# A two-branch transformer step on one core: narrower modulation tiles, and a last norm on one engine

## The chip, the core and the metric

The kernel runs on one core of one Trainium2 chip. The core has five engines with instruction streams of their own: TensorE (PE; its weight loads are shown as PEld), VectorE (DVE), ScalarE (ACT), GpSimd (POOL) and SyncE (SP), which here only issues transfers; they wait for each other through semaphores. The metric is the device time in microseconds (us). The kernel before took 1598.36 us, the median of 3 runs (1598.06 to 1599.08).

## What is computed

One layer of a hybrid model is applied to 128 context tokens and 512 latent tokens, 640 rows of 1024 columns in fp32. A conditioning vector for each of the two kinds gives six modulation vectors. Cut to what matters here:

```python
def _layer(x, cond, p, lb, s0):
    mod = jax.nn.silu(cond) @ p['w_ada'] + p['b_ada']          # 1024 -> 6 x 1024
    sh1, sc1, g1, sh2, sc2, g2 = jnp.split(mod[:, None, :], N_MOD, axis=-1)
    mix, s_out = _token_mixer(x * (1 + sc1) + sh1, p, lb, s0)  # conv, gated scan, chunk gating; then W_o
    x = _layernorm(DEEPNORM_ALPHA * x + g1 * mix, p['ln1_g'], p['ln1_b'])
    ffn = _swiglu(x * (1 + sc2) + sh2, p['w_ffn_in'], p['w_ffn_out'])   # 1024 -> 2 x 2816 -> 1024
    x = _layernorm(DEEPNORM_ALPHA * x + g2 * ffn, p['ln2_g'], p['ln2_b'])
    return x, s_out
```

`_layernorm` subtracts the row mean, divides by the row's standard deviation and applies a gain and an offset per column.

## The kernel before

**Products.** Every large product is made of three fp32r matmuls: a weight tile is split into a rounded part (`wh`, ScalarE, L199) and a rest (`wl`, VectorE or POOL, L200), the activations likewise (`split`, L384 on ScalarE and L385 on VectorE), and `mm3` (L216 to L218) or `mm3t` (L221 to L223) multiplies high by high, high by low and low by high into one PSUM tile. The weights come through one queue (L174, on SP) a few tiles ahead.

**Order of the work.** Most of the program is traced as interleaved generators; a scheduler then sets the order on each engine from its own estimates. Where the code stands in `with in_order()`, the instructions of VectorE, ScalarE and POOL keep the order of the program.

**Stages.** The first stage computes four of the twelve 512-column slices of the modulation (L570) while the first weights load. The second, 60 to about 500 us, runs the input projection and the gated scan, and between them the other eight slices, `ada_slice(n)` for n = 4 to 11. Each slice multiplies `silu(cond)` (1024 values for two kinds of token, held as 128x32 blocks, `sil`) by 1024x512 of `w_ada`. `ada_small` (L716) loads it as four tiles of 2 blocks of 128 rows by 512 columns through two buffers (L719, on SP). The matmul (L422) of row block k writes 32 PSUM partitions, at 32 * (k % 4), so the four partition groups collect partial sums of blocks 0 to 3 and then 4 to 7:

```python
j = kc % 4
last = PE.matmul(ps[32 * j:32 * j + 32, :], sil[:, kc, :], t[:, k, :], start=kc < 4, stop=kc >= 4)
```

Then `ada_fin` copies the sum to SBUF, adds the groups by a small matmul (L433 or L439) and adds the bias.

**First norm.** From about 1100 us `o2(t)` computes the second half of the output projection of the 128-row block t (five blocks), adds the residual (L1160, L1161), takes statistics (L1430, L1431) and a reciprocal square root by three Newton steps (`rsqrt_col`, L114 to L122), and gives `nb` (L1434). `x1_apply(t)` normalizes the block on ScalarE (L1439), `x1t(t)` transposes it on TensorE (L1451) and scales it (L1464), followed by the split. In the loop `x1t(t - 1)` follows `o2(t)`.

**Feed-forward part.** `hidden` computes the gated hidden units in groups (its matmuls are L1527 to L1529; `p`, `u` and `fsg` are its intermediate tiles). One step of the generator `x1_resid` is drawn per group: the first scales gain and offset of the first norm by ALPHA (`lgb`, called l1gb in the profile, 128x2048, L1655), and each of five applies them to a block of the residual (`rr`, L1657, L1658).

**Tail.** The last part of the second product runs block by block. `evac` multiplies the PSUM tile by the gate (`rt`, L1693), adds it to `rr` (L1694) and takes statistics (L1696). Then the block's norm follows: mean and variance (L1734), Newton steps, `nb` (L1744), and for each 512-column half either two passes on VectorE (L1741, L1753) or, for six of the ten halves (`by_pool`), one on ScalarE (L1749) and two on POOL (L1750, L1751). Each half is stored by its own transfer (L1755). The scheduler orders the tail.

## Time and profile before

The profiled execution took 1599.31 us (a span of 1597.5 us on the core); the runs' median is 1598.36 us.

| Engine | busy us | share | instructions |
|---|---|---|---|
| PE (TensorE) | 1550.9 | 97% | 10846 |
| DVE (VectorE) | 1148.4 | 72% | 1971 |
| ACT (ScalarE) | 513.5 | 32% | 799 |
| POOL (GpSimd) | 192.3 | 12% | 182 |

148.30 MB moved at a mean of 93 GB/s. The mean granted clock of TensorE was 0.994 of full speed.

How its lines are read: a timeline row gives the start in us, the duration, the engine, the line, the operation, the tile written and those read, the shape and the number of instructions in the row; in brackets stands how long the engine had been idle before, and what released it. Matmuls overlap, so the time one takes from the next is the distance of their starts. A line of waits gives who waited for whom, the total, the number and the longest. In the order rows a matmul counts once where the profile has two records for plain fp32 operands.

### The profile page before, as it was taken

How to read it: one execution, taken by the hardware profiler on the slowest of the kernel's cores; microseconds unless marked ns; L12 is line 12 of the kernel's file. 1: busy time of each engine (PE TensorE's matmuls, PEld its weight loads, DVE VectorE, ACT ScalarE, POOL GpSimd, SP SyncE). 2: the span in 40 equal slices, each digit the busy share in tenths (PEclk: the TensorE clock that was granted, in tenths of full speed). 3: DMA queues.
4: the chain of work that ended last, by engine and by line, in shares of the span. 5: the costliest groups of instructions: out<-in, count | busy, mean ns of one | idle time of the engine just before them, and what ended most of it. 6: DMA issues, size and time to landing. Idle time of an engine off the chain costs nothing.

```text
span 1597.5 us, 26110 instructions
## 1 busy us (share of the span) xinstructions
PE 1550.9 (97%) x10846; PEld 1422.4 (89%) x10846; DVE 1148.4 (72%) x1971; ACT 513.5 (32%) x799; POOL 192.3 (12%) x182
## 2 busy tenths in 40 slices
PE   7999999999999999999999999999899999999995
PEld 4988998888887899999999899997788898898984
DVE  5555456565677999988997563377896685685878
ACT  3333333233333221121222343223643243242441
POOL 1120220322300000000002312430000000000014
PEclk9999999999999999999999999999899999999998
DMA  9632333333222322322222123432133222223221
GB/s 321 207 106 87 88 98 100 99 94 100 70 58 81 91 80 67 89 70 78 68 67 67 53 80 106 159 93 66 48 111 119 66 80 98 62 80 93 62 85 66
DMA packets 197014, 148.30 MB, mean 93 GB/s; under 512 B 4945, under 2 KB 174441, under 8 KB 196640
## 3 DMA queue, kind: packets, MB, share of 16 engines
q1 hardware_dynamic: 195984, 145.24, 30.2%
q8 instruction: 85, 1.39, 0.4%
q10 hardware_dynamic: 912, 1.39, 0.2%
q14 instruction: 33, 0.27, 0.1%
HBM read 140.31 MB, written 6.31 MB: 92 GB/s over the span
## 4 chain that ended last, share of the span: by engine, by line
PE 84%; DVE 7%; DMA 5%; ACT 2%; issue 1%; POOL 0%; SPq 0%; ACTq 0%; DVEq 0%
PE mm L216 15%; PE mm L218 15%; PE mm L217 15%; PE fx L1527 3%; PE fx L1529 3%; PE fx L1528 3%; PE lv L810 3%; PE fy L1527 2%; PE fo L221 2%; PE fo L222 2%; PE fo L223 2%; PE fy L1529 2%; PE fy L1528 2%; DMA adaw<-in_w_ada_dram 2%; PE vps L221 2%; PE vps L223 2%
## 5 line engine op out<-in xcount | busy, mean ns | idle before, releaser
L216 PE MATMUL mm<-mH,wh 128*128 128x320 f32 x1280 | 401.8, 314 | 0.0
L217 PE MATMUL mm<-mL,wh 128*128 128x320 f32 x1280 | 396.4, 310 | 0.0
L218 PE MATMUL mm<-mH,wl 128*128 128x320 f32 x1280 | 396.1, 309 | 0.0
L199 ACT CAST wh<-raw 128x1024 fp32r<-128x1024 f32 (+1 forms) x186 | 185.0, 995 | 534.7 <-PE mm L217 358.4
L200 DVE TENSOR_TENSOR wl<-raw,wh 128x1024 fp32r<-128x1024 f32 (+1 forms) x185 | 220.6, 1193 | 140.2 <-ACT wh L199 140.0
L216 PEld LDWEIGHTS mm<-mH,wh 128*128 128x128 f32 x1280 | 240.3, 188 | 9.0 <-issue 5.5
L217 PEld LDWEIGHTS mm<-mL,wh 128*128 128x128 f32 x1280 | 240.4, 188 | 3.6 <-issue 3.6
L218 PEld LDWEIGHTS mm<-mH,wl 128*128 128x128 f32 x1280 | 240.3, 188 | 0.3
L997 DVE SCALAR_TENSOR_TENSOR ca<-hb,convw,ca 128x328 f32<-128x328 f32 x464 | 229.0, 560 | 0.0
L1527 PE MATMUL fy<-mT,wh 128*128 128x320 f32 x264 | 85.1, 323 | 3.8 <-ACT p L1541 2.5
L1529 PE MATMUL fy<-mT,wl 128*128 128x320 f32 x264 | 83.6, 316 | 0.4 <-DVE wl L200 0.4
L1528 PE MATMUL fy<-mT,wh 128*128 128x320 f32 x264 | 83.0, 315 | 0.3 <-DVE mT L1519 0.3
L199 ACT CAST wh<-S 128x1024 fp32r<-128x1024 f32 x43 | 44.9, 1050 | 91.2 <-issue 34.7
L221 PE MATMUL vps<-wh,mH 128*128 128x256 f32 (+1 forms) x200 | 66.6, 334 | 0.0
L200 POOL TENSOR_TENSOR wL<-raw,wL 128x1024 fp32r<-128x1024 f32 (+1 forms) x3 | 6.8, 2280 | 494.1 <-ACT wL L199 489.5
L223 PE MATMUL vps<-wh,mL 128*128 128x256 f32 (+1 forms) x200 | 65.7, 328 | 0.0
L222 PE MATMUL vps<-wl,mH 128*128 128x256 f32 (+1 forms) x200 | 65.5, 328 | 0.0
L200 DVE TENSOR_TENSOR wl<-S,wh 128x1024 fp32r<-128x1024 f32 x43 | 52.6, 1222 | 17.5 <-ACT wh L199 17.5
L754 POOL TENSOR_SCALAR fT<-fT,oml,lb 128x640 f32<-128x640 f32 x16 | 26.1, 1632 | 322.6 <-ACT fT L751 270.2
L832 DVE TENSOR_TENSOR k<-k,t 128x320 f32<-128x320 f32 x40 | 21.8, 546 | 55.1 <-PE lv L810 54.8
L1527 PEld LDWEIGHTS fy<-mT,wh 128*128 128x128 f32 x264 | 50.7, 192 | 8.5 <-ACT p L1541 5.4
L1527 PE MATMUL fx<-mB,wh 128*128 128x320 f32 x176 | 55.1, 313 | 2.0 <-ACT u L1604 1.3
(406 smaller groups left out, 3413.1 us busy)
## 6 DMA issues: line engine op xcount, KB each, us to landing
raw<-in_w_in_dram SPq DMA_DIRECT2D x96, 512.0 KB
adaw<-in_w_ada_dram SPq DMA_DIRECT2D x48, 512.0 KB
raw<-in_w_ffn_in_dram SPq DMA_DIRECT2D x44, 512.0 KB
raw<-in_w_ffn_out_dram SPq DMA_DIRECT2D x20, 512.0 KB
raw<-in_w_b_out_dram SPq DMA_DIRECT2D x8, 512.0 KB
raw<-in_w_c_out_dram SPq DMA_DIRECT2D x8, 512.0 KB
raw<-in_w_a_out_dram SPq DMA_DIRECT2D x8, 512.0 KB
raw<-in_w_o_dram SPq DMA_DIRECT2D x8, 512.0 KB
```

The costliest lines, as they stand in the source:

```text
L199: S_.copy(h, raw)
L200: le.tensor_tensor(out=lo, in0=raw, in1=h.bitcast(F32), op=ALU.subtract)
L216: PE.matmul(ps, h, aH, start=first, stop=False)
L217: PE.matmul(ps, h, aL, start=False, stop=False)
L218: return PE.matmul(ps, lo, aH, start=False, stop=last)
L221: PE.matmul(ps, aH, h, start=first, stop=False)
L222: PE.matmul(ps, aH, lo, start=False, stop=False)
L223: return PE.matmul(ps, aL, h, start=False, stop=last)
L997: paced(V_.scalar_tensor_tensor(out=ca[:, p_], in0=hb[:, p_.start + j:p_.stop + j], scalar=convw[:, k, j:j + 1], in1=ca[:, p_], op0=ALU.mu ...
L1527: PE.matmul(ps, wh, bh, start=kc == 0 and not add, stop=False, skip_group_check=add)
L1528: PE.matmul(ps, wh, bl, start=False, stop=False, skip_group_check=add)
L1529: PE.matmul(ps, wl, bh, start=False, stop=kc == 3, skip_group_check=add)
```

## The change

It has four parts.

1. **Modulation slices of the second stage.** A tile is now four row blocks by 256 columns, [128, 4, 256] for [128, 2, 512], and each tile's four matmuls, 32x256, go to the four partition groups. There are still four loads of 512 KB a slice, two buffers and the same totals; the rows of a load are 1 KB for 2 KB.
2. **First norm.** `x1t(0)` is called in the middle of `o2(2)`, behind four of its eight k blocks, and not behind `o2(1)`.
3. **l1gb.** The scaling by ALPHA is a ScalarE activation; the constraint that put it behind the last instruction of the stretch in order is gone, and the first draw of the generator is left out, so the residual blocks follow one group later.
4. **Last norm.** All halves are normalized on VectorE, in steps: `rsqrt_col` is now a generator (with the multiplication by -0.5 ahead of the first guess), and `norm2(t)` yields between its steps. `evac` of the next block draws up to three steps after each of its instructions. The tail stands in `in_order()`, so VectorE keeps this order. POOL and ScalarE do nothing there but ScalarE's part of the transfers.

```diff
--- before.py
+++ after.py
@@ -107,18 +107,26 @@
             V_.scalar_tensor_tensor(out=dst, in0=u, scalar=1.5, in1=dst, op0=ALU.add, op1=ALU.mult)
             yield
 
...
+        yield
         V_.tensor_scalar(out=u.bitcast(I32), in0=x[:, 0:1].bitcast(I32), scalar1=1, scalar2=None,
                          op0=ALU.logical_shift_right)
+        V_.tensor_scalar(out=x[:, 1:2], in0=x[:, 0:1], scalar1=-0.5, scalar2=None, op0=ALU.mult)
+        yield
         V_.tensor_scalar(out=dst.bitcast(I32), in0=u.bitcast(I32), scalar1=-1.0, scalar2=float(MAGIC),
                          op0=ALU.mult, op1=ALU.add)
-        V_.tensor_scalar(out=x[:, 1:2], in0=x[:, 0:1], scalar1=-0.5, scalar2=None, op0=ALU.mult)
         for _ in range(3):
+            yield
             V_.tensor_scalar(out=u, in0=dst, scalar1=dst, scalar2=x[:, 1:2], op0=ALU.mult, op1=ALU.mult)
+            yield
             V_.scalar_tensor_tensor(out=dst, in0=u, scalar=1.5, in1=dst, op0=ALU.add, op1=ALU.mult)
 
     def ln_stats(pool, src, mean, rstd, tag):
@@ -409,19 +417,12 @@
 
     def ada_slice(n, pmp, loads, pool, tag):
 
-        fin = ada_mm(n, pmp, loads, pool, tag)[1]
-        fin()
-
-    def ada_mm(n, pmp, loads, pool, tag):
         ps = pmp.tile([P, 512], F32, tag="pm", name="mods")
-        last = None
-        for t, k0, kcs in loads(n):
-            for k in range(kcs):
-                kc = k0 + k
-                j = kc % 4
-                last = PE.matmul(ps[32 * j:32 * j + 32, :], sil[:, kc, :], t[:, k, :],
-                                 start=kc < 4, stop=kc >= 4)
-        return last.ins, lambda: ada_fin(n, ps, pmp, pool, tag)
+        for t, c0, k0 in loads(n):
+            for j in range(4):
+                PE.matmul(ps[32 * j:32 * j + 32, c0:c0 + 256], sil[:, k0 + j, :], t[:, j, :],
+                          start=k0 == 0, stop=k0 == 4)
+        ada_fin(n, ps, pmp, pool, tag)
 
...
@@ -714,11 +715,12 @@
...
     def ada_small(n):
-        for k0 in range(0, KC, 2):
-            t = hp.tile([P, 2, 512], F32, tag="adw", name="adaw2", bufs=2)
-            SP.dma_start(t, w_ada[k0 * P:(k0 + 2) * P, n * 512:(n + 1) * 512].rearrange(
-                "(k p) n -> p k n", p=P))
-            yield t, k0, 2
+        for c0 in (0, 256):
+            for k0 in (0, 4):
+                t = hp.tile([P, 4, 256], F32, tag="adw", name="adaw2", bufs=2)
+                SP.dma_start(t, w_ada[k0 * P:(k0 + 4) * P, n * 512 + c0:n * 512 + c0 + 256].rearrange(
+                    "(k p) n -> p k n", p=P))
+                yield t, c0, k0
 
     def ada_op(n):
         def f():
@@ -1416,7 +1418,7 @@
     xH, xL = X()
...
-    def o2(t):
+    def o2(t, mid=None):
         tsl = slice(t * P, (t + 1) * P)
         ps = newps("ops2")
         stt = st["lbs"][:, t]
@@ -1424,6 +1426,8 @@
         nn = 512 if t < NT - 1 else 256
         for c in range(0, 512, nn):
             for k in range(KC):
+                if k == 4 and mid:
+                    mid()
                 mm3t(ps[:, 0, c:c + nn], oH[:, k, c:c + nn], oL[:, k, c:c + nn], xH[:, k, tsl], xL[:, k, tsl],
                      k == 0, k == KC - 1)
             resid(t, 512 + c, nn, ps[:, 0, c:c + nn], g1b)
@@ -1470,8 +1474,8 @@
 
     w_need(3)
     for t in range(NT - 1):
-        x1_apply(t, o2(t))
-        if t:
+        x1_apply(t, o2(t, (lambda: x1t(0)) if t == 2 else None))
+        if t > 1:
             x1t(t - 1)
     order = in_order()
     order.__enter__()
@@ -1651,8 +1655,7 @@
 
     def x1_resid():
 
-        with tc.issue_after(last.ins):
-            V_.tensor_scalar(out=lgb, in0=lgb, scalar1=ALPHA, scalar2=None, op0=ALU.mult)
+        S_.activation(lgb, lgb, AF.Copy, scale=ALPHA)
         for t in range(NT):
             V_.tensor_tensor(out=rr[:, t], in0=rr[:, t], in1=lgb[:, 0], op=ALU.mult)
             V_.tensor_tensor(out=rr[:, t], in0=rr[:, t], in1=lgb[:, 1], op=ALU.add)
@@ -1660,6 +1663,14 @@
 
     x1r = x1_resid()
     st2 = pe.tile([P, NT, 3, 6], F32, name="st2")
+    norms = []
+
+    def norm_steps(n):
+        while n and norms:
+            n -= 1
+            if next(norms[0], True):
+                norms.pop(0)
+
...
@@ -1675,7 +1686,8 @@
                 hH.append(hs[:, 2 * k - 4])
                 hL.append(hs[:, 2 * k - 3])
             left = hidden(hH[k], hL[k], early.pop(0) if early else None, left)
-            next(x1r, None)
+            if part or k:
+                next(x1r, None)
             gate.clear()
         left()
         if part == 0:
@@ -1688,12 +1700,15 @@
             SP.dma_start(lgb2[:, 1], bcast_row(ln2_b[0]))
         final = part == len(PARTS) - 1
 
-        def evac(t, ps, n0, nn):
+        def evac(t, ps, n0, nn, steps=0):
             tmp = pe.tile([P, nn], F32, tag="rt", name="rt2")
             V_.tensor_tensor(out=tmp, in0=ps, in1=g2b[:, min(t, 1), n0:n0 + nn], op=ALU.mult)
+            norm_steps(steps)
             V_.tensor_tensor(out=rr[:, t, n0:n0 + nn], in0=rr[:, t, n0:n0 + nn], in1=tmp, op=ALU.add)
+            norm_steps(steps)
             if final:
                 V_.bn_stats(st2[:, t, {512: 0, 768: 1}.get(n0, 2)], rr[:, t, n0:n0 + nn])
+            norm_steps(steps)
 
...
-    by_pool = ((0, 0), (1, 0), (2, 0), (2, 1), (3, 0), (3, 1))
-    w_take(2 * len(L_KCS))
-    for t in range(NT):
...
-        for i in cols_:
-            for kc in range(HH - 1 if t == 0 else 0, HH):
-                prod(*i, kc)
-            evac(t, ps[i[0]], *i)
+    def norm2(t):
         mv = pe.tile([P, 2], F32, tag="mv", name="mv2", bufs=2)
         V_.bn_aggr(mv, st2[:, t] if t == NT - 1 else st2[:, t, 0::2])
+        yield
         rs = pe.tile([P, 1], F32, tag="rs2", name="rs2", bufs=2)
-        rsqrt_col(pe, rs, mv[:, 1:2], tag="ln2")
-        for hf in range(2):
+        xs = [rr[:, t, hf * 512:(hf + 1) * 512] for hf in range(2)]
+        for i, _ in enumerate(rsqrt_col_g(pe, rs, mv[:, 1:2], tag="ln2")):
+            if i in (1, 3):
+                V_.scalar_tensor_tensor(out=xs[i // 2], in0=xs[i // 2], scalar=mv[:, 0:1],
+                                        in1=lgb2[:, 0, i // 2 * 512:(i // 2 + 1) * 512], op0=ALU.subtract, op1=ALU.mult)
+            yield
+        dst = y_prompt[0] if t == 0 else y_sample[0, (t - 1) * P:t * P, :]
+        for hf, x in enumerate(xs):
             sl = slice(hf * 512, (hf + 1) * 512)
-            x = rr[:, t, sl]
-            if (t, hf) not in by_pool:
-                V_.scalar_tensor_tensor(out=x, in0=x, scalar=mv[:, 0:1], in1=lgb2[:, 0, sl],
-                                        op0=ALU.subtract, op1=ALU.mult)
-        nb = pe.tile([P, 1], F32, tag="nb2", name="nb2", bufs=2)
-        V_.scalar_tensor_tensor(out=nb, in0=mv[:, 0:1], scalar=-1.0, in1=rs, op0=ALU.mult, op1=ALU.mult)
-        for hf in range(2):
-            sl = slice(hf * 512, (hf + 1) * 512)
-            x = rr[:, t, sl]
-            if (t, hf) in by_pool:
-                S_.activation(x, x, AF.Identity, scale=rs, bias=nb)
-                G_.tensor_tensor(out=x, in0=x, in1=lgb2[:, 0, sl], op=ALU.mult)
-                G_.tensor_tensor(out=x, in0=x, in1=lgb2[:, 1, sl], op=ALU.add)
-            else:
-                V_.scalar_tensor_tensor(out=x, in0=x, scalar=rs, in1=lgb2[:, 1, sl], op0=ALU.mult, op1=ALU.add)
-            dst = y_prompt[0] if t == 0 else y_sample[0, (t - 1) * P:t * P, :]
+            yield
+            V_.scalar_tensor_tensor(out=x, in0=x, scalar=rs, in1=lgb2[:, 1, sl], op0=ALU.mult, op1=ALU.add)
             (SP if hf else S_).dma_start(dst[:, sl], x)
+
+    w_take(2 * len(L_KCS))
+    with in_order():
+        for t in range(NT):
...
+            for i in cols_:
+                for kc in range(HH - 1 if t == 0 else 0, HH):
+                    prod(*i, kc)
+                evac(t, ps[i[0]], *i, 0 if t == NT - 1 and i[0] == 768 else 3)
+            norms.append(norm2(t))
+        norm_steps(1000)
 
 
 # ---- launch: one core; inputs and outputs as the reference has them ----
```

TensorE at the third and fourth tile of the first slice (`adaw` is a tile of w_ada, `mods` the slice's PSUM tile), before:

```order
L216 MATMUL mm<-mH,wh 128x320
L422 MATMUL mods<-adaw_971,sil 32x512 x2
L217 MATMUL mm<-mL,wh 128x320
L218 MATMUL mm<-mH,wl 128x320
L216 MATMUL mm<-mH,wh 128x320
L217 MATMUL mm<-mL,wh 128x320
L218 MATMUL mm<-mH,wl 128x320
L422 MATMUL mods<-adaw_975,sil 32x512 x2
L810 MATMUL lv<-q_850,k_710 64x64 x10
```

and in the change:

```order
L224 MATMUL mm<-mH,wh 128x320
L423 MATMUL mods<-adaw_975,sil 32x256 x4
L225 MATMUL mm<-mL,wh 128x320
L226 MATMUL mm<-mH,wl 128x320
L224 MATMUL mm<-mH,wh 128x320
L225 MATMUL mm<-mL,wh 128x320
L226 MATMUL mm<-mH,wl 128x320
L224 MATMUL mm<-mH,wh 128x320
L225 MATMUL mm<-mL,wh 128x320
L423 MATMUL mods<-adaw_981,sil 32x256 x4
```

Each lone tile has four narrow matmuls for two wide ones; the third tile stands three matmuls earlier, and seven matmuls lie between the two for five.

VectorE at the scaling of l1gb (`S` are sums of weight tiles, `hp` the rest of a hidden group, `u` and `fsg` the group's gate), before:

```order
L200 TENSOR_TENSOR wl<-S_10987,wh 128x1024
L1655 TENSOR_SCALAR l1gb<-l1gb 128x2048
L1590 TENSOR_TENSOR u_10874<-u_10874,fy 128x320
L1657 TENSOR_TENSOR rr<-rr,l1gb 128x1024
L1591 TENSOR_TENSOR fsg<-fsg,u_10874 128x320
L1658 TENSOR_TENSOR rr<-rr,l1gb 128x1024
L385 TENSOR_TENSOR hp<-fsg,hp 128x640
L1211 TENSOR_TENSOR S_11089<-raw 128x512
L1212 TENSOR_TENSOR S_11089<-raw 128x512
L200 TENSOR_TENSOR wl<-raw,wh 128x1024
```

and in the change:

```order
L208 TENSOR_TENSOR wl<-S_11051,wh 128x1024
L1594 TENSOR_TENSOR u_10938<-u_10938,fy 128x320
L1595 TENSOR_TENSOR fsg<-fsg,u_10938 128x320
L1660 TENSOR_TENSOR rr<-rr,l1gb 128x1024
L393 TENSOR_TENSOR hp<-fsg,hp 128x640
L1213 TENSOR_TENSOR S_11150<-raw 128x512
L1214 TENSOR_TENSOR S_11150<-raw 128x512
L208 TENSOR_TENSOR wl<-raw,wh 128x1024
```

The scaling and one of the two passes over `rr` are gone from ahead of `hp` and `wl`. On ScalarE, in the same place, the scaling now stands ahead of the rounding of `hp` and of the next `wh`:

```order
L207 CAST wh<-S_11051 128x1024
L1658 ACTIVATE l1gb<-l1gb 128x2048
L392 CAST hp<-fsg 128x640
L207 CAST wh<-raw 128x1024
L1545 COPY p_11174<-fx 128x320
L1545 COPY p_11189<-fy 128x320
```

Before, it read there:

```order
L199 CAST wh<-S_10987 128x1024
L1541 COPY p_11113<-fx 128x320
L199 CAST wh<-raw 128x1024
L1541 COPY p_11128<-fy 128x320
L199 CAST wh<-raw 128x512
L384 CAST hp<-fsg 128x640
```

The two copies and the smaller rounding come later in exchange, and `hp` earlier.

VectorE in the tail, from the first column half of block 1 to the second (`st` are statistics, `mv` mean and variance of block 0, `rs` its reciprocal root), before:

```order
L1693 TENSOR_TENSOR rt_14610<-fo,g2b 128x512
L1734 BN_AGGR mv_14570<-st_10995 128x2
L1694 TENSOR_TENSOR rr<-rr,rt_14610 128x512
L114 TENSOR_SCALAR ln2x<-mv_14570 128x1
L1741 SCALAR_TENSOR_TENSOR rr<-rr,mv_14570,l2gb 128x512
L115 TENSOR_SCALAR ln2u<-ln2x 128x1
L119 TENSOR_SCALAR ln2x<-ln2x 128x1
L1696 BN_STATS st_10995<-rr 128x6
L117 TENSOR_SCALAR rs_14572<-ln2u 128x1
L121 TENSOR_SCALAR ln2u<-rs_14572,ln2x 128x1
L122 SCALAR_TENSOR_TENSOR rs_14572<-ln2u,rs_14572 128x1
```

and in the change:

```order
L1705 TENSOR_TENSOR rt_14650<-fo,g2b 128x512
L1728 BN_AGGR mv_14652<-st_11059 128x2
L118 TENSOR_SCALAR ln2x<-mv_14652 128x1
L120 TENSOR_SCALAR ln2u<-ln2x 128x1
L122 TENSOR_SCALAR ln2x<-ln2x 128x1
L1734 SCALAR_TENSOR_TENSOR rr<-rr,mv_14652,l2gb 128x512
L1707 TENSOR_TENSOR rr<-rr,rt_14650 128x512
L124 TENSOR_SCALAR rs_14654<-ln2u 128x1
L128 TENSOR_SCALAR ln2u<-rs_14654,ln2x 128x1
L1734 SCALAR_TENSOR_TENSOR rr<-rr,mv_14652,l2gb 128x512
L130 SCALAR_TENSOR_TENSOR rs_14654<-ln2u,rs_14654 128x1
L1710 BN_STATS st_11059<-rr 128x6
```

A second pass (L1734) stands where POOL had one, and the short steps are spread between the long ones; the last two passes (L1741) of block 0 come behind the next `rt`.

More of the change, by code (lines that the diff above doesn't have):

```diff
@@ L108, in rsqrt_g, with rsqrt_col, rsqrt_col_g @@
             yield
-    def rsqrt_col(pool, dst, var, tag):
+    def rsqrt_col(*a, **k):
+        for _ in rsqrt_col_g(*a, **k):
+            pass
+    def rsqrt_col_g(pool, dst, var, tag):
         x = pool.tile([P, 2], F32, tag=tag + "x", name=tag + "x")
@@ L1708, in hybrid_step @@
                         evac(t, slot[t], hf * 512, 512)
-    by_pool = ((0, 0), (1, 0), (2, 0), (2, 1), (3, 0), (3, 1))
-    w_take(2 * len(L_KCS))
-    for t in range(NT):
-        tsl = slice(t * P, (t + 1) * P)
-        cols_ = [(512, 512), (0, 512)]
-        if t == NT - 1:
-            cols_ = [(0, 512), (512, 256), (768, 256)]
-        ps = {n0: bank("fo")[:, 0:nn] for n0, nn in cols_}
-        def prod(n0, nn, kc):
-            o = n0 % 512
-            h, lo = [w[:, kc, o:o + nn] for w in st[f"wL{n0 // 512}"]]
-            mm3t(ps[n0], h, lo, hH[kc][:, tsl], hL[kc][:, tsl], kc == 0, kc == HH - 1)
-        if t == 0:
-            for i in cols_:
-                for kc in range(HH - 1):
-                    prod(*i, kc)
-        for i in cols_:
-            for kc in range(HH - 1 if t == 0 else 0, HH):
-                prod(*i, kc)
-            evac(t, ps[i[0]], *i)
+    def norm2(t):
@@ new lines, in hybrid_step, with prod @@
+    w_take(2 * len(L_KCS))
+    with in_order():
+        for t in range(NT):
+            tsl = slice(t * P, (t + 1) * P)
+            cols_ = [(512, 512), (0, 512)]
+            if t == NT - 1:
+                cols_ = [(0, 512), (512, 256), (768, 256)]
+            ps = {n0: bank("fo")[:, 0:nn] for n0, nn in cols_}
+            def prod(n0, nn, kc):
+                o = n0 % 512
+                h, lo = [w[:, kc, o:o + nn] for w in st[f"wL{n0 // 512}"]]
+                mm3t(ps[n0], h, lo, hH[kc][:, tsl], hL[kc][:, tsl], kc == 0, kc == HH - 1)
+            if t == 0:
+                for i in cols_:
+                    for kc in range(HH - 1):
+                        prod(*i, kc)
+            for i in cols_:
+                for kc in range(HH - 1 if t == 0 else 0, HH):
+                    prod(*i, kc)
+                evac(t, ps[i[0]], *i, 0 if t == NT - 1 and i[0] == 768 else 3)
+            norms.append(norm2(t))
+        norm_steps(1000)
```

## Prediction

> **What bounds the kernel now.** I read the page first: the span, and the engines' shares of the chain that ended last.
>
> ```profile
> span 1597.5 us, 26110 instructions
> PE 84%; DVE 7%; DMA 5%; ACT 2%; issue 1%; POOL 0%; SPq 0%; ACTq 0%; DVEq 0%
> ```
>
> TensorE (PE) carries the chain, so a TensorE microsecond saved, or an idle one closed, comes off the end, except where another engine ends last. Four stretches of the view by windows (length; busy PE, PEld, DVE, ACT, POOL; granted clock; DMA share; GB/s) show where that is.
>
> ```profile
> 10.00:45.00 35.00, 30.97 (x233) 20.59 (x236) 23.09 (x68) 12.07 (x22) 3.91 (x5) 1.00 1.09 353
> 300.00:400.00 100.00, 98.47 (x930) 87.36 (x928) 57.41 (x94) 34.70 (x67) 21.23 (x22) 1.00 0.32 96
> 500.00:700.00 200.00, 200.00 (x1251) 190.85 (x1250) 193.99 (x418) 45.15 (x50) 1.25 (x15) 1.00 0.27 77
> 1545.00:1598.00 53.00, 35.45 (x164) 28.17 (x162) 45.84 (x106) 7.57 (x11) 21.78 (x14) 0.91 0.14 50
> ```
>
> The first is bound by loads, the second and the third (like nearly all of 60 to 1545) by TensorE, the last by VectorE. The change touches stretches of the last two kinds, so each part needs its own ruler. TensorE's waits that bear on it:
>
> ```profile
> PE mods L422 <- DMA adaw<-in_w_ada_dram: 3.8, 7, 2.0
> PE fo L221 <- DVE rt L1693: 2.7, 5, 0.9
> ```
>
> **Part 1, modulation slices.** TensorE's timeline at the first of the eight slices, one later tile, and a visit of the first stage:
>
> ```profile
> 36.28 1.93 PE L570 MATMUL mods<-adaw,sil 128*32 128x256 f32 x32
> 38.14 0.51 PE L648 MATMUL v0a<-wh,mH 128*128 128x256 f32 x2
> ...
> 89.20 1.07 PE L422 MATMUL mods<-adaw,sil 128*32 128x512 f32 x8
> ...
> 94.27 1.05 PE L422 MATMUL mods<-adaw,sil 128*32 128x512 f32 x4
> 95.25 0.41 PE L217 MATMUL mm<-mL,wh 128*128 128x320 f32 x1
> ...
> 96.18 1.05 PE L422 MATMUL mods<-adaw,sil 128*32 128x512 f32 x4
> ...
> 299.40 1.05 PE L422 MATMUL mods<-adaw,sil 128*32 128x512 f32 x4 [1.97 <-DMA adaw<-in_w_ada_dram]
> ```
>
> An instruction leaves two records here, so x8 is the pair of tiles at a slice's start (four instructions, one on each 32-column position), and x4 a tile alone: two instructions on two positions. The pair takes 1.07 and the lone tile 1.05: half the work for the same time. The first stage shows the new shape, 32x256 on all four positions: x32 is 16 instructions, four tiles' worth, and 38.14 - 36.28 = 1.86 us, so 0.465 a tile, where a lone tile now holds TensorE 95.25 - 94.27 = 0.98. All eight slices have two lone tiles; the number of visits stays. Saved: 16 x (0.98 - 0.465) = 8.2; with the pair as the ruler (half of 1.07 less the 0.07 of overlap, 0.50) 16 x 0.48 = 7.7. I take 7.7.
>
> What can take some back is the loads. Two buffers serve four tiles, so the third and the fourth load wait until TensorE has released the first and the second. In the changed order the third tile stands three 128x320 matmuls earlier, but the first tile is released after one of the pair's two halves, some 0.5 us earlier: even. The second is released when it was; the fourth tile is reached by TensorE about 0.5 (shorter third) + 0.15 (two matmuls fewer ahead of it) earlier. How much room there is shows the DMA view of 88 to 100 us, 0.3 us a digit:
>
> ```profile
> DMA  0000020000093998999998200000569899410001
> ```
>
> The third and fourth tile's bytes move from 91.3 to about 94.9, and the fourth is used at 96.18: 1.3 us of room, less 0.65. The rows of a load become 1 KB instead of 2 KB. The 10 to 45 us stretch, where slices with 1 KB rows load beside weights with shorter ones, moved 353 GB/s; two tiles are 1.05 MB, 3.0 us by that, inside the 3.7 that the pair takes here. Seven waits already stand at these tiles, 3.8 us in all, among them the 1.97 in the last row. In that slice (the fifth) one matmul of the first tile was placed 30 us ahead; now the whole first tile and one matmul of the second are, so only the fourth load still waits for a late release and that 1.97 stays about what it is. At the other six places TensorE comes up to 0.65 earlier: 6 x 0.2 for half of them or so, 1.2. **Sum -6.5**; bounds -8.2 (nothing given back) and -3 (0.3 us at all 16 lone tiles, 4.7).
>
> The Trainium skill (DMA: Bandwidth & Descriptors, Specifications) puts the smallest transfer for line rate at 512 B; by it rows of 1 KB cost nothing and this part would be -7.7 or more. The 353 GB/s agrees as far as it goes.
>
> **Part 2, the transposes of block 0 one block later.** TensorE, VectorE and ScalarE there:
>
> ```profile
> 1107.24 1.24 ACT L1439 ACTIVATE rr<-rr,nb,rstd 128x1024 f32<-128x1024 f32 x1 [10.89 <-DVE nb L1434]
> 1108.53 1.09 PE L1451 MATMUL x1T<-ident,rr 128*128 128x128 f32 x8 [1.30 <-ACT rr L1439]
> ...
> 1111.62 0.16 DVE L1434 SCALAR_TENSOR_TENSOR nb<-lbm,rstd 128x1 f32<-128x1 f32 x1
> ...
> 1121.45 1.09 PE L1451 MATMUL x1T<-ident,rr 128*128 128x128 f32 x8
> ```
>
> TensorE stood 1.30 for ScalarE's normalization of block 0. With the transposes seven matmuls later that wait goes. But block 1's transposes keep their place, and need block 1's normalization: nb at 1111.62 comes at the end of a VectorE sequence that runs without a gap from 1107 and doesn't start earlier. 1111.62 + 0.2 + 1.24 puts them at about 1113.1, where TensorE arrives at 1112.5: half the stall is back there, and block 2's (1121.45) hang on VectorE, which now has block 0's split between. **Sum 0**, bounds -1.3 (the whole stall) and +0.5.
>
> **Part 3, scaling l1gb on ScalarE.** The three engines at the start of the feed-forward part:
>
> ```profile
> 1158.12 1.23 DVE L1655 TENSOR_SCALAR l1gb<-l1gb 128x2048 f32<-128x2048 f32 x1 [0.24 <-DMA l1gb<-in_ln_b_dram]
> ...
> 1162.96 0.83 DVE L385 TENSOR_TENSOR hp<-fsg,hp 128x640 fp32r<-128x640 f32 x1 [0.54 <-ACT hp L384]
> ...
> 1164.91 1.22 DVE L200 TENSOR_TENSOR wl<-raw,wh 128x1024 fp32r<-128x1024 f32 x1
> 1160.41 1.05 ACT L199 CAST wh<-raw 128x1024 fp32r<-128x1024 f32 x1 [0.19 <-DMA raw<-in_w_ffn_in_dram]
> 1161.51 0.41 PE L1527 MATMUL fx<-mB,wh 128*128 128x320 f32 x1 [0.29 <-ACT wh L199]
> 1166.18 0.42 PE L1529 MATMUL fx<-mB,wl 128*128 128x320 f32 x1 [2.03 <-DVE wl L200]
> ```
>
> TensorE stands 2.03 for wl, the end of the VectorE queue. Out of that queue go the scaling (1.23) and one of the two rr passes ahead of it (the first call of the generator is skipped, so one full-width pass of 1.22 moves behind). ScalarE gets 128x2048: twice the 1.24 of its 128x1024, less one fixed part, 2.3 us, from about 1158.1 (landing of l1gb) to 1160.4. Then come hp (0.73), wh (1.05, done 1162.0 instead of 1161.4: TensorE's 0.29 wait grows by 0.6). VectorE waits for the scaled l1gb, runs one rr pass 1160.45 to 1161.6, then hp, two sums, and wl from 1163.55 to 1164.75, where it was 1164.91 to 1166.13. TensorE's 2.03 shrinks to what is left behind the grown wait; it goes on at 1164.8 instead of 1166.18. The moved pass falls in a stretch with VectorE slack. **Sum -1.35**; bounds -2.0 (all of the wait) and +0.7 (ScalarE's queue slips and wl gains nothing).
>
> **Part 4, last norm on VectorE.** VectorE's timeline at the tail, POOL's row beside it:
>
> ```profile
> 1556.16 0.69 DVE L1693 TENSOR_TENSOR rt<-fo,g2b 128x512 f32<-128x512 f32 x1
> ...
> 1557.57 0.74 DVE L1741 SCALAR_TENSOR_TENSOR rr<-rr,mv,l2gb 128x512 f32<-128x512 f32 x1
> ...
> 1560.44 0.16 DVE L122 SCALAR_TENSOR_TENSOR rs<-ln2u,rs 128x1 f32<-128x1 f32 x1
> ...
> 1562.09 1.48 DVE L1694 TENSOR_TENSOR rr<-rr,rt 128x512 f32<-128x512 f32 x1
> ...
> 1564.21 0.67 DVE L1693 TENSOR_TENSOR rt<-fo,g2b 128x512 f32<-128x512 f32 x1
> ...
> 1579.80 0.67 DVE L1693 TENSOR_TENSOR rt<-fo,g2b 128x512 f32<-128x512 f32 x1
> ...
> 1586.40 0.24 DVE L1734 BATCH_NORM_AGGREGATE mv<-st 128x2 f32<-128x18 f32 x1
> ...
> 1587.53 1.63 DVE L1741 SCALAR_TENSOR_TENSOR rr<-rr,mv,l2gb 128x512 f32<-128x512 f32 x1
> ...
> 1589.56 0.73 DVE L122 SCALAR_TENSOR_TENSOR rs<-ln2u,rs 128x1 f32<-128x1 f32 x1
> ...
> 1590.63 0.88 DVE L122 SCALAR_TENSOR_TENSOR rs<-ln2u,rs 128x1 f32<-128x1 f32 x1
> ...
> 1591.85 0.99 DVE L122 SCALAR_TENSOR_TENSOR rs<-ln2u,rs 128x1 f32<-128x1 f32 x1
> ...
> 1592.96 1.41 DVE L1753 SCALAR_TENSOR_TENSOR rr<-rr,rs,l2gb 128x512 f32<-128x512 f32 x2
> 1561.72 1.30 POOL L1750 TENSOR_TENSOR rr<-rr,l2gb 128x512 f32<-128x512 f32 x1 [10.20 <-ACT rr L1749]
> ```
>
> VectorE runs from block to block without a gap: 8.05 us from block 1 to block 2, (1579.80 - 1564.21) / 2 = 7.80 after. While POOL works, instructions of VectorE with two operands from SBUF take twice as long: 1.48 for a 0.69 sum, 1.63 for a 0.74 one. The change adds two half-block passes (0.65 each at their cadence), takes away nb (0.08) and the slowing (1.48 - 0.69 = 0.79): 8.05 + 0.43 = 8.5 a block; as the short rsqrt steps now stand between long passes and no longer wait for one another, I take 8.25. The last block starts 8.05 + 15.6 - 3 x 8.25 = 1.1 us late; in it VectorE also has the four passes of block 3, which POOL did: 4 x 0.65, less about 0.4 for one slowed sum, part of which covered short steps. So its statistics end 1.1 + 2.2 = 3.3 late. The final chain was 1594.37 - 1586.40 = 7.97, of which 0.89 is the slowed pass and 2.1 the three slowed Newton steps (0.73, 0.88 and 0.99 for 0.16): 4.95 without POOL, 3.0 less. **Sum +0.3**, bounds -2 (the passes hide all rsqrt waits) and +2 (8.5 a block, and no more from the last).
>
> **Total** -6.5 + 0 - 1.35 + 0.3 = -7.5. The profiled execution took 1599.31 us, 0.95 above the median of the runs, so 1591.8 for such an execution and 1590.9, say **1591**, for the median. About 0.2% (3.2 us) can be told from no change.
>
> **Rivals.** *The loads take the gain (16%).* If the fourth tile's load isn't covered, the gain of the slice turns into the wait beside 299.40: with 0.3 us at each of 16 tiles and parts 3 and 4 at their middle it is 1598.4 - 3 - 1.05 = 1594.3; with part 3's gain lost too, 1595.7. For it: seven waits are there already. Against: 1.3 us of room in the slice shown.
>
> *The loads overturn it (4%).* One mechanism on the other side: each lone tile waits like the one at 299.40, and the weight loads queued behind it on SP come late. It decides from 16w = 3.8 + 7.7 + 1.1 + 3.2, so w = 1 us per lone tile; at the full 1.97 the result is 1598.4 - 7.7 - 1.1 + 31.5 - 3.8, 1617. Against it: the DMA share of 0.32 at 300 to 400 us, and no wait for weights in that stage.
>
> *The clock decides (8%).* TensorE's granted clock falls after idle stretches in the feed-forward start:
>
> ```profile
> 1155.00:1160.00 5.00, 4.74 (x23) 4.74 (x24) 4.76 (x7) 0.89 (x2) 0.00 (x0) 0.68 1.05 321
> ```
>
> A stretch like this one loses 5 x 0.32 = 1.6 us. Parts 2 and 3 move its idle gaps: with two stretches more the result is 1594, with this one gone 1589. The Trainium skill (TensorE: Matmul & The Clock Gate, Part 1) has the gate look through a free-running window, so every earlier microsecond could shift which gap trips it. The runs of before lie within 1.0 us, which speaks against large luck.
>
> *Everything lands (13%).* No wait for loads, block 0's stall gone for good, VectorE's tail 2 shorter: -8.2 - 1.3 - 1.35 - 2, about 1586.
>
> *Tail at its bad end (6%)*, VectorE at 8.5 or more a block: 1593.
>
> **Chances.** The forecast, between 1588.5 and 1593.5, has 53%. Faster by more than 0.2% (below 1595.2) come the forecast, the full gain, 0.06 of the clock's 0.08, 0.04 of the tail's 0.06 and a quarter of the first rival: 0.53 + 0.13 + 0.06 + 0.04 + 0.04 = 0.80. Within 0.2% come the rest of that rival and 0.02 of clock and tail: 0.14. Slower are the overturn and what is left of clock and tail: 0.06. The range 1586 to 1596.5 leaves out the full overturn and a tenth at the ends.
>
> **What would show it.** Part 1: rows of 32x256 x8 (a lone tile) of about 0.5 us and waits for adaw in all below 6 us; wrong if those waits pass 8. Part 2: the 1.30 is gone, and a stall of about 0.6 stands at block 1's transposes. Part 3: wl's 2.03 falls below 0.8, and wh's 0.29 grows. Part 4: no POOL row behind 1552, no sum over 0.8 us on VectorE there, blocks 8.2 to 8.5 apart, a final chain near 5 us. The forecast fails if the span from 60 to 500 us shortens by less than 4 us.

## The result

The changed kernel took 1588.55 us (median of 4 runs, 1587.7 to 1590.29), the kernel before beside it 1598.21: a ratio of 0.9939 with a 95% interval of 0.9927 to 0.9952, that is 7.7 to 11.7 us less. Measured again beside two variants of it, it was 0.9931 (0.9918 to 0.9943). The forecast was 1591, 7.4 us less, with a range of 1586 to 1596.5.

The page of the changed kernel, the same two lines as before:

```profile
span 1587.1 us, 26350 instructions
PE 86%; DVE 7%; DMA 4%; ACT 2%; issue 1%; POOL 0%; ACTq 0%; DVEq 0%
```

The share of loads in the chain fell by one point, and TensorE's rose. To see where the 10.4 us of span went, I cut both traces at the starts of the same instructions and take the difference of the lengths: the first matmul of the gated scan (`lv`), the first of the output projection (`ops`), the first of the feed-forward part (`fx`), the first of its second product (`fo`), the last of its first product (`fx` or `fy`), and the end. The other columns are runs of the experiments below, each with one part alone; each column is a single execution.

| stretch, us | before | after | part 1 alone | part 2 alone | part 3 alone | part 4 alone |
|---|---|---|---|---|---|---|
| start to first lv | 80.90 | 79.80 | 79.85 | 80.27 | 80.39 | 79.98 |
| to first ops (slices) | 1014.16 | 1007.25 | 1007.10 | 1013.42 | 1014.98 | 1015.53 |
| to first fx (first norm) | 29.73 | 29.64 | 29.60 | 29.43 | 29.14 | 29.57 |
| to first fo (l1gb) | 94.59 | 92.56 | 94.42 | 94.34 | 91.41 | 93.17 |
| to last fx or fy | 325.00 | 324.58 | 324.58 | 325.16 | 325.14 | 325.18 |
| to the end (tail) | 53.16 | 53.30 | 53.06 | 53.09 | 53.06 | 53.29 |

The second row carries 6.9 of the 10.4 us, the fourth 2.0, the first 1.1 (code that the change doesn't touch), the fifth 0.4, and the tail gives back 0.1. The terms of the four parts can thus be read apart, which totals that spread over some microseconds don't allow.

**Part 1.** TensorE's timeline at the first slice and at one later third tile, then its waits:

```profile
88.10 1.07 PE L423 MATMUL mods<-adaw,sil 128*32 128x256 f32 x16
...
92.64 0.64 PE L423 MATMUL mods<-adaw,sil 128*32 128x256 f32 x8
93.21 0.41 PE L225 MATMUL mm<-mL,wh 128*128 128x320 f32 x1
...
391.20 0.64 PE L423 MATMUL mods<-adaw,sil 128*32 128x256 f32 x8 [1.36 <-DMA adaw<-in_w_ada_dram]
```

```profile
PE mods L423 <- DMA adaw<-in_w_ada_dram: 2.6, 3, 1.4
PE x1T L1455 <- ACT rr L1443: 1.2, 2, 0.7
```

A lone tile holds TensorE 93.21 - 92.64 = 0.57 us where it held it 0.98; the pair stays at 1.07. Summed over all visits, without the waits ahead of them, the slices hold TensorE 17.5 us for 24.4. The waits for loads didn't grow: seven of 3.8 us became three of 2.6.

**Part 2.** Block 0's transposes and those of block 1 and 2, with the normalization that block 1's wait for:

```profile
1100.66 1.04 PE L1455 MATMUL x1T<-ident,rr 128*128 128x128 f32 x8
...
1103.64 0.16 DVE L1438 SCALAR_TENSOR_TENSOR nb<-lbm,rstd 128x1 f32<-128x1 f32 x1
1103.84 1.24 ACT L1443 ACTIVATE rr<-rr,nb,rstd 128x1024 f32<-128x1024 f32 x1 [1.30 <-DVE nb L1438]
...
1105.14 1.09 PE L1455 MATMUL x1T<-ident,rr 128*128 128x128 f32 x8 [0.71 <-ACT rr L1443]
...
1113.37 1.09 PE L1455 MATMUL x1T<-ident,rr 128*128 128x128 f32 x8 [0.46 <-ACT rr L1443]
```

The stall of 1.30 at block 0 is gone, and 0.71 and 0.46 stand at the next two: 1.17 in all. ScalarE itself waits 1.30 for `nb`, so it is VectorE's statistics that set this pace, and they weren't moved.

**Part 3.** ScalarE, VectorE and TensorE where l1gb is scaled:

```profile
1149.79 1.92 ACT L1658 ACTIVATE l1gb<-l1gb 128x2048 f32<-128x2048 f32 x1 [2.09 <-DMA l1gb<-in_ln_b_dram]
...
1152.23 1.04 ACT L207 CAST wh<-raw 128x1024 fp32r<-128x1024 f32 x1
1154.82 1.22 DVE L208 TENSOR_TENSOR wl<-raw,wh 128x1024 fp32r<-128x1024 f32 x1
1153.32 0.42 PE L1531 MATMUL fx<-mB,wh 128*128 128x320 f32 x1 [0.33 <-ACT wh L207]
...
1156.13 0.38 PE L1533 MATMUL fx<-mB,wl 128*128 128x320 f32 x1
```

The wait of 2.03 us for `wl` is gone altogether, and the one for `wh` is 0.33 where it was 0.29.

**Part 4.** VectorE at the first product sum of blocks 1, 2 and 4, the last statistics, and the last two passes:

```profile
1545.55 0.69 DVE L1705 TENSOR_TENSOR rt<-fo,g2b 128x512 f32<-128x512 f32 x1
...
1553.80 0.67 DVE L1705 TENSOR_TENSOR rt<-fo,g2b 128x512 f32<-128x512 f32 x1
...
1570.28 0.67 DVE L1705 TENSOR_TENSOR rt<-fo,g2b 128x512 f32<-128x512 f32 x1
...
1579.07 0.24 DVE L1728 BATCH_NORM_AGGREGATE mv<-st 128x2 f32<-128x18 f32 x1
...
1582.54 1.42 DVE L1741 SCALAR_TENSOR_TENSOR rr<-rr,rs,l2gb 128x512 f32<-128x512 f32 x2
```

Blocks are 8.25 us apart (8.24 each on to block 4), and the final chain is 1583.96 - 1579.07 = 4.89 us for 7.97.

### The profile page after: what moved, and what is told of

The parts are those of the page before. It is cut to its first block, busy times and chain, and to the rows that moved or that the text cites. A ratio compares the mean times of both kernels' runs of the same rounds, so it can differ in the third digit from the quotient of the medians.

```text
span 1587.1 us, 26350 instructions
## 1 busy us (share of the span) xinstructions
PE 1543.0 (97%) x10974; PEld 1423.8 (90%) x10974; DVE 1148.4 (72%) x1977; ACT 510.2 (32%) x794; POOL 173.8 (11%) x170
## 4 chain that ended last, share of the span: by engine, by line
PE 86%; DVE 7%; DMA 4%; ACT 2%; issue 1%; POOL 0%; ACTq 0%; DVEq 0%
PE mm L224 15%; PE mm L226 15%; PE mm L225 15%; PE fx L1531 3%; PE fx L1533 3%; PE lv L812 3%; PE fx L1532 3%; PE fy L1531 3%; PE fo L229 2%; PE fo L230 2%; PE fo L231 2%; PE fy L1533 2%; PE fy L1532 2%; PE vps L229 2%; PE vps L230 2%; PE vps L231 2%
## 5 line engine op out<-in xcount | busy, mean ns | idle before, releaser
L208 DVE TENSOR_TENSOR wl<-S,wh 128x1024 fp32r<-128x1024 f32 x43 | 52.5, 1222 | 17.5 <-ACT wh L207 17.5
```

Of the source, the lines that this page charges most:

```text
L208: le.tensor_tensor(out=lo, in0=raw, in1=h.bitcast(F32), op=ALU.subtract)
```

## The experiments

### Each part alone

The kernel before with only the hunks of one part from the diff above. Part 1:

> The kernel before with part 1 alone (modulation tiles of 4 blocks by 256 columns). My theory: the gain of part 1 is TensorE time, since a lone tile now fills four 32-column positions; in the two traces the start of the output projection moved by 8.0 us, 1.1 of it already ahead of the first slice, so this kernel should be 6.9 us faster than before (5.9 to 7.5), with all modulation matmuls holding TensorE about 17.5 us for 24.4. Rival (the loads take part of it, or part of the 9.7 us comes from elsewhere): 3 to 5 us faster.

Measured: 1590.40 us beside 1597.92, ratio 0.9951 (0.9938 to 0.9964), 5.8 to 9.9 us faster. Its visits hold TensorE 17.5 us, its waits for loads are 2.6, and the second row of the table moved as in the full change. The rival of 3 to 5 us is out; most of what the change brings is this part.

Part 3:

> The kernel before with part 3 alone (l1gb scaled on ScalarE, first draw left out). My theory: the wait of TensorE for wl (2.03 us) goes and nothing comes in its place: 1.4 to 2.4 us faster, 2.0 by the traces. Rival (the 0.65 us beyond the prediction came from the granted clock, which happens to be 1.00 in place of 0.71 in one 5 us stretch, and not from this part): 1.3 us faster or less, and the low clock in that stretch stays.

Measured: 1595.76, ratio 0.9984 (0.9975 to 0.9992), 1.3 to 4.0 us faster. TensorE's view of waits has the answer:

```profile
PE fx L1529 <- DVE wl L200: 0.4, 1, 0.4
```

The 2.0 us is gone here, and stands in the three other kernels of this set. The part has two edits, and no run tells them apart. In the program with the scaling alone, which was not run, the second pass over `rr` still stands between `hp` and `wl` on VectorE; with the first draw left out as well it comes behind `wl`. By that order the missing draw bears about one pass (1.22) of the gain, an estimate that no run tests. The fourth row of the table is 3.2 us shorter than before's, more than the wait. That is the rival's half of the truth: how long this stretch is also depends on how often TensorE's clock fell in it (below).

Part 4:

> The kernel before with part 4 alone (last norm on VectorE, no POOL). My theory: the statistics of the last block come 3.3 us later and the final chain is 3.1 us shorter: 0 to 0.5 us slower. Rival (the relief from POOL pays by itself): 1 to 2 us faster. Second rival (VectorE's extra passes decide): 1 to 2 us slower.

Measured: 1598.31, ratio 0.9999 (0.9990 to 1.0007). The totals leave room from 1.6 us less to 1.1 us more, but the tail of 53.29 us stands against 53.06 to 53.16 in the four kernels without part 4: 0.1 to 0.2 us longer. Neither rival holds.

Part 2:

> The kernel before with part 2 alone (block 0's transposes in the middle of block 2's product). My theory: TensorE's stall of 1.30 us at block 0 comes back as two stalls, 0.5 to 0.7 us each, and the third block's transposes start when they did: 0.1 us faster, within 0.3 us of before. Rival (the stall is gone for good): 1 to 1.3 us faster.

Measured: 1598.09, ratio 0.9997 (0.9988 to 1.0006). Its trace has the waits of 0.49 and 0.46 at blocks 1 and 2 and none at block 0. The stretch is 29.43 us, inside the 29.14 to 29.73 of the kernels in the table without it. No effect can be told. Over all traces in this document the stretch has a mean of 29.15 us in the six with part 2 and 29.41 in the seven without, so part 2 may bring 0.3 us, within their spread.

### One position for both matmuls of a tile

```diff
-                j = kc % 4
-                last = PE.matmul(ps[32 * j:32 * j + 32, :], sil[:, kc, :], t[:, k, :],
-                                 start=kc < 4, stop=kc >= 4)
+        for t, j in loads(n):
+            for k in range(2):
+                last = PE.matmul(ps[32 * j:32 * j + 32, :], sil[:, 4 * k + j, :], t[:, k, :],
+                                 start=k == 0, stop=k == 1)
...
+        w4 = w_ada.rearrange("(k j p) n -> p k j n", j=4, p=P)
+        for j in range(4):
...
+            SP.dma_start(t, w4[:, :, j, n * 512:(n + 1) * 512])
```

> The kernel before with the same loads' size and the same 512-column matmuls, but each tile holds row blocks j and j + 4, so that both matmuls of a tile go to the same 32-column position j, one after the other. My theory (TensorE's time at a tile is the longest string of matmuls on one position): a lone tile takes 1.96 us for 0.98 and the pair of tiles 1.96 for 1.00, so 16 x 0.98 + 8 x 0.96 = 23 us slower, less what the waits for loads (4.0 us) give back: 19 to 24 us slower. Rival (a tile costs what its columns and instructions cost, wherever they are put): within 2 us of before.

Measured: 1619.89, ratio 1.0132 (1.0116 to 1.0147), 18.5 to 23.5 us slower. TensorE at the first slice:

```profile
89.74 1.92 PE L420 MATMUL mods<-adaw,sil 128*32 128x512 f32 x8
...
96.41 1.90 PE L420 MATMUL mods<-adaw,sil 128*32 128x512 f32 x4 [0.89 <-DMA adaw<-in_w_ada_dram]
98.24 0.41 PE L217 MATMUL mm<-mL,wh 128*128 128x320 f32 x1
```

The same two matmuls hold TensorE 98.24 - 96.41 = 1.83 us instead of 0.98, and the pair of tiles 1.92 instead of 1.07. The cost of a tile is the longest string of matmuls on one 32-column position, which is what part 1 halves.

### Narrower still: eight blocks by 128 columns

From part 1's code:

```diff
-        for t, c0, k0 in loads(n):
-            for j in range(4):
-                PE.matmul(ps[32 * j:32 * j + 32, c0:c0 + 256], sil[:, k0 + j, :], t[:, j, :],
-                          start=k0 == 0, stop=k0 == 4)
+        for t, c0 in loads(n):
+            for kc in range(KC):
+                j = kc % 4
+                PE.matmul(ps[32 * j:32 * j + 32, c0:c0 + 128], sil[:, kc, :], t[:, kc, :],
+                          start=kc < 4, stop=kc >= 4)
...
+        for c0 in range(0, 512, 128):
+            t = hp.tile([P, KC, 128], F32, tag="adw", name="adaw2", bufs=2)
+            SP.dma_start(t, w_ada[:, n * 512 + c0:n * 512 + c0 + 128].rearrange("(k p) n -> p k n", p=P))
+            yield t, c0
```

> The kernel before with modulation tiles of 8 row blocks by 128 columns: four loads of 512 KB a slice as before, rows of 512 B, eight 32x128 matmuls to a tile, two on each of the four positions. My theory: the positions are as full as in part 1, so TensorE's time is that of part 1 (0.57 a lone tile) and the kernel 7 us faster than before, unless narrow matmuls cost more than half of 256 columns: 5 to 7.5 us faster; waits for adaw stay below 5 us. Rival (the row length sets the rate of the load): waits for adaw of 10 us or more at the 16 lone tiles, 3 us faster or slower than before.

Measured: 1594.86, ratio 0.9977 (0.9968 to 0.9986), 2.2 to 5.1 us faster: less than the theory asked for, and a miss. The rival missed too: it asked for waits of 10 us, and they are 4.9. TensorE's time is as expected, 18.1 us in all visits and 0.57 a lone tile. The rest is in the waits and in the clock. Waits, then the seventh slice in the timeline and by windows (the last three columns of a window are granted clock, DMA share and GB/s):

```profile
PE mods L416 <- DMA adaw<-in_w_ada_dram: 4.9, 7, 1.7
```

```profile
395.36 0.64 PE L416 MATMUL mods<-adaw,sil 128*32 128x128 f32 x16 [1.73 <-DMA adaw<-in_w_ada_dram]
...
397.92 1.08 PE L416 MATMUL mods<-adaw,sil 128*32 128x128 f32 x16
```

```profile
395.30:399.50 4.20, 4.14 (x41) 3.12 (x41) 0.00 (x0) 0.43 (x1) 0.00 (x0) 0.60 0.04 12
```

The waits are 2.3 us above those of part 1 alone (2.0 to 4.0 in the six traces with part 1's tiles), and after the longest of them TensorE ran at a granted clock of 0.60 for some 4 us, where the fourth tile took 1.08 and not 0.64: 4.2 x 0.4 = 1.7 us more. That stretch belongs to the profiled execution; how many of the ten runs had one is not shown. The loads themselves are slower with shorter rows. The same transfer pair (third and fourth tile of the first slice) in the view of transfers, GB/s in 40 steps of 0.3 us (12 us from 88.0, 86.9 and 87.9), with rows of 2 KB, 1 KB and 512 B, so for the kernel before, the changed one and this one:

```profile
GB/s 0 0 0 0 0 55 0 0 0 0 0 137 82 239 273 300 375 410 382 423 416 314 109 34 0 0 0 0 109 195 266 242 375 365 154 55 0 0 0 20
```

```profile
GB/s 0 0 0 0 0 55 0 0 0 17 154 184 280 345 389 355 352 362 352 365 225 68 24 24 0 0 0 3 96 198 290 331 389 324 130 0 0 75 242 259
```

```profile
GB/s 0 0 0 0 55 0 0 0 0 29 147 157 265 311 350 347 343 333 290 297 287 224 111 7 0 0 0 7 123 184 283 365 386 324 143 0 0 24 162 225
```

The five to eight full steps have a mean of 401, 360 and 320 GB/s. Other loads share these steps, so the figures are rough, but the order is the one the rival asked for: the row length sets the rate, only at a smaller price in waits than it gave. The Trainium skill (DMA: Bandwidth & Descriptors, Specifications) gives 512 B as the smallest transfer for line rate; here the rows of 512 B stay a fifth below those of 2 KB.

### The last norm with POOL's work left out

```diff
-                G_.tensor_tensor(out=x, in0=x, in1=lgb2[:, 0, sl], op=ALU.mult)
-                G_.tensor_tensor(out=x, in0=x, in1=lgb2[:, 1, sl], op=ALU.add)
```

> The kernel before with POOL's two passes over six halves of the last norm left out (gain and offset of these halves are not applied), all else in its order. My theory: POOL slows VectorE's passes with two operands from SBUF, 0.8 us in each of blocks 1 and 2, 1 and 0.9 in the last two, 3.0 in the final chain; TensorE hides part of it: 5 to 6.5 us faster than before, the final chain 5.0 for 7.97 us. Rival (those passes are slow for their own reasons or wait for something else): less than 1.5 us faster and the final chain over 7 us.

Measured: 1591.72, ratio 0.9958 (0.9944 to 0.9971), and the tail 46.60 us for 53.16. VectorE's last chain:

```profile
1582.49 0.24 DVE L1734 BATCH_NORM_AGGREGATE mv<-st 128x2 f32<-128x18 f32 x1
...
1583.61 0.74 DVE L1741 SCALAR_TENSOR_TENSOR rr<-rr,mv,l2gb 128x512 f32<-128x512 f32 x1
...
1586.05 1.41 DVE L1751 SCALAR_TENSOR_TENSOR rr<-rr,rs,l2gb 128x512 f32<-128x512 f32 x2
```

The pass that took 1.63 takes 0.74, and the chain is 1587.46 - 1582.49 = 4.97 us for 7.97. So 6.6 us is what POOL's twelve passes cost the kernel before, though POOL never ends the chain itself; the change takes this off and pays about as much for doing their work on VectorE.

### Part of the norm back on POOL

The changed kernel with a list of halves that go to ScalarE and POOL as before, in the order of the steps; the last block always stays on VectorE.

```diff
+    by_pool = ((0, 0), (1, 0), (2, 0), (2, 1))
...
-            if i in (1, 3):
+            if i in (1, 3) and (t, i // 2) not in by_pool:
...
+            if (t, hf) in by_pool:
+                S_.activation(x, x, AF.Identity, scale=rs, bias=nb)
+                G_.tensor_tensor(out=x, in0=x, in1=lgb2[:, 0, sl], op=ALU.mult)
+                G_.tensor_tensor(out=x, in0=x, in1=lgb2[:, 1, sl], op=ALU.add)
+            else:
+                yield
+                V_.scalar_tensor_tensor(out=x, in0=x, scalar=rs, in1=lgb2[:, 1, sl], op0=ALU.mult, op1=ALU.add)
```

Four halves:

> The changed kernel with the last norm of four halves (block 0 and 1 the first half, block 2 both) given back to ScalarE and POOL, block 3 and 4 staying on VectorE, in the order of the steps. My theory: a half on POOL saves VectorE 1.3 us of passes and costs it 0.8 of slowing and 0.1 for nb, 0.4 a half, and the final chain stays free of POOL: 1 to 1.7 us faster than the changed kernel, 10.7 to 11.4 faster than before. Rival (in this order more of VectorE's passes meet POOL): 0 to 2 us slower than the changed kernel, that is 7.7 to 9.7 faster than before.

Measured: 1589.54, ratio 0.9938 (0.9926 to 0.9951), tail 53.30 us as in the changed kernel: the rival held, not the theory. The gain of blocks 1 to 3 (the last block starts 3.0 us earlier in the tail) is lost in the last block, where block 2's two halves keep POOL busy:

```profile
1571.84 1.68 DVE L1734 SCALAR_TENSOR_TENSOR rr<-rr,mv,l2gb 128x512 f32<-128x512 f32 x1
1573.44 1.21 DVE L130 SCALAR_TENSOR_TENSOR rs<-ln2u,rs 128x1 f32<-128x1 f32 x1
...
1571.70 1.26 POOL L1745 TENSOR_TENSOR rr<-rr,l2gb 128x512 f32<-128x512 f32 x1 [1.31 <-ACT rr L1744]
1573.05 1.59 POOL L1746 TENSOR_TENSOR rr<-rr,l2gb 128x512 f32<-128x512 f32 x1
```

Then two halves, (0, 0) and (1, 0):

> The changed kernel with only the first half of blocks 0 and 1 given back to ScalarE and POOL. My theory after the run with four halves (there block 3's first product sum was evacuated 1.45 us earlier after the end of the feed-forward matmuls than in the changed kernel, and POOL's halves of block 2 then cost block 3 and 4 all of it): these two halves keep their 1.4 us, since POOL is done before the last block: 1.4 us faster than the changed kernel. Rival (VectorE's slowed passes travel with POOL's whichever half it is): the same time as the changed kernel, within 0.5 us in the stretch from the last feed-forward matmul to the end, 53.3 us.

Measured: 1587.82, ratio 0.9927 (0.9915 to 0.9940), tail 52.37 us, 0.9 less. Three halves, with (2, 0):

> The changed kernel with the first half of blocks 0, 1 and 2 given back to ScalarE and POOL. My theory: the third half saves 0.7 us of passes in block 3 beyond the slowing and then slows one pass and some Newton steps of block 3's norm in the last block by 1 to 1.7 us: 0.5 to 1.5 us faster than the changed kernel, not faster than with two halves. Rival: each half on POOL pays 0.7 us: 2.1 us faster than the changed kernel.

Measured: 1586.95, ratio 0.9926 (0.9913 to 0.9940), tail 51.69 us, 1.6 less. And the changed kernel once more beside these two:

> The changed kernel again, beside the two others on one chip. My theory: 9 to 10 us faster than before, the stretch from the last feed-forward matmul to the end 53.3 us, with the stretch ahead of the first gated-scan matmul varying by 1 us either way. Rival (the 1.1 us that the first trace gained ahead of the changed stages belongs to the change): that stretch is again 79.8 us and the kernel 10 us or more faster.

Measured: 1587.55, ratio 0.9931 (0.9918 to 0.9943), tail 53.29, and the first stretch 80.44 us: the 1.1 us ahead of the slices is chance, not the change. The total is 11.0 us below the kernel before, above the 9 to 10 that I had expected.

By the tail alone the order is three halves, two, none or four. I had expected two to gain 1.4 and three no more than two, and missed both: the first two halves brought 0.9 together and the third 0.7, until a block has both its halves there. By the totals, 1586.95, 1587.82 and 1587.55, the three can't be told apart. The version with three halves has the lowest median of all that ran, and only the trace says that it is faster.

## Why the prediction was right

**Part 1: direction and cause right, and the size met with some luck.** The term said -6.5: 7.7 from TensorE, 1.2 given back at the loads. The two profiled runs differ by 6.9 in this stretch, but no term is as forecast. A lone tile takes 0.57 and not 0.50, since the time around a visit (0.10 of it) doesn't shrink with the tile: 16 x 0.41 = 6.6, and with the fifth slice, whose matmuls are placed otherwise, 6.9 in place of 7.7. The loads gave nothing back: the waits for them fell by 1.2 us. I had taken TensorE's earlier arrival at the fourth tile as a loss. But a wait is left only where the release of a buffer comes late, and fewer places had that: three waits for seven. Rows of 1 KB cost 10% of rate, which the room of 1.3 us probably covered. In the other direction goes a term that the sum lacks: TensorE's busy time in the stretch fell by only 5.8 us (1008.36 to 1002.58 in the view by windows), so its other products took 1.1 us more in the changed order; what holds them up stays open.

Eleven traces give the size: from the first `lv` to the first `ops` it is 1013.4 to 1016.3 us in five kernels with before's tiles and 1006.7 to 1008.8 in six with part 1's, and the means, 1014.9 and 1007.4, differ by 7.5. But three of the five hold a stretch of 3.4 us at half the clock behind the wait at the fifth slice (shown in the last section), 1.7 us each, and none of the six does. The two that don't hold one are 6.4 above the six. The wait there, for which the prediction left 1.97, is 1.05 in the changed kernel; whether that keeps the clock up or chance does, the runs don't show.

**Part 2: right.** The sum of 0 was -0.1, with the stall back at block 1 as reckoned (0.71 for "half"), and a second piece at block 2. In the repeat of the changed kernel only 0.4 us of waits stood there, and the stretch took 28.67, so the stall itself varies from one execution to the next.

**Part 3: mechanism right, size too small.** -1.35 was forecast; from `fx` to `fo` the traces with one low stretch of the clock take 93.0 to 93.2 us without the part and 91.3 to 91.5 with it, those with two 94.3 to 94.4 and 92.4 to 92.6: -1.7 to -1.9. The term that was mis-sized is ScalarE's pass, 2.3 us by twice the 128x1024 row less one fixed part; it took 1.92. With that `wh` is hardly later (0.33 for a forecast 0.9; 0 to 0.84 in the six traces with the part), and `wl` is done just when TensorE comes.

**Part 4: right.** +0.3 was forecast, +0.1 to +0.2 measured; the blocks are 8.25 apart as taken, and the chain 4.89 for 4.95. That VectorE takes twice as long beside POOL is better read as a wait for POOL's instruction to end (last section); the sum stands, since it was added up from measured rows.

**The rivals.** The loads neither took the gain nor overturned it. The clock was a rival with 1.6 us a stretch, and it accounts for part of the spread: the same kernel's stretch from `fx` to `fo` comes out in two lengths. Two traces of the changed kernel show it, at the same distance from the first `fx` (windows; granted clock is the third column from the end):

```profile
1130.69:1134.69 4.00, 2.80 (x11) 2.58 (x12) 3.92 (x7) 1.38 (x3) 0.00 (x0) 0.73 0.00 0
```

```profile
1130.71:1134.71 4.00, 2.29 (x13) 1.80 (x13) 3.92 (x7) 1.86 (x5) 0.00 (x0) 1.00 0.00 0
```

The first is the profiled run of the result (92.56 us from `fx` to `fo`), the second the repeat (91.50). The kernel before, in its profiled run, had a longer one in the same place, with this window in it:

```profile
1142.79:1146.79 4.00, 3.48 (x13) 3.08 (x13) 2.89 (x4) 3.52 (x6) 0.00 (x0) 0.50 0.00 0
```

So the kernel before had more of the low clock there than the changed one, and of the 2.0 us of that row in the table 1.7 to 1.9 are part 3's, by the kernels that are alike in this; the 1.1 us ahead of the slices belongs to no part. The prediction put little on chance because three runs of the kernel before lay within 1.0 us; 27 runs of it beside the single parts go from 1595.5 to 1601.4. The Trainium skill (TensorE: Matmul & The Clock Gate, Part 1) says that the gate judges activity in a free-running window; two executions of one program that differ in this way agree with it, though no run here shows what starts a low stretch.

**The total.** By traces that are alike in the clock the parts come to 6.4 to 6.9, at most 0.3, 1.7 to 1.9, and 0.1 to 0.2 back: 8 to 9 us for a forecast of 7.5. The medians are 9.7 and 11.0 us apart in the two sets. The rest lies in pieces such as the clock and the first stretch, and 0.6 us in the fifth row: 324.3 to 324.7 in the six kernels with part 1 and 325.0 to 325.2 in the five with before's tiles, for which no cause is shown. That 1588.55 lies inside 1588.5 to 1593.5 is in part luck; the repeat, 1587.55, lies below it.

## What to carry to other kernels

Matmuls with 32 output columns cost, in these traces, by the longest string on one column position: shape the tiles of such a product so that every tile that may come alone fills all positions. An engine that never ends the chain can still be the cost, here POOL's passes that held up VectorE's; leave work out once to see that price before moving it. Where runs spread as much as an edit is worth, cut the traces at the same instructions and compare stretches: a tail's 0.1 to 0.2 us could be read where totals leave over 1 us open.
